# One residue of an output-projection weight block: VectorE subtraction in place of a scaled copy and an adding DMA

## The chip, the cores and the metric

The kernel runs on one core of one Trainium2 chip. The metric is device time in microseconds (us); lower is better. The core has five engines that follow their own instruction streams and meet through semaphores: TensorE (PE in the profile, with its weight loads under PEld), VectorE (DVE), ScalarE (ACT), GpSimd (POOL) and SyncE (SP, which only issues DMAs here). DMAs that SP issues are on the hardware queue q1 in the profile, those that GpSimd issues on the software queue q0.

## What is computed

One layer of a streaming-encoder block on 512 frames of width 1024, all in float32:

```
h = h + 0.5 * swiglu_1(rmsnorm(h))
z = rmsnorm(h) @ w_in          -> conv value, conv gate, q, k, v, r, forget gate
y_conv = silu(layernorm(causal depthwise conv, 31 taps, of value * sigmoid(gate)))
y_gla  = chunked gated linear attention (chunks of 64), normed, gated by silu(r)
h = h + concat([y_conv, y_gla]) @ w_out        # w_out is 1024 x 1024
h = h + 0.5 * swiglu_2(rmsnorm(h))
h = h + sigmoid(rmsnorm(h) @ w_g) * (p @ w_p)
out = rmsnorm(h)
```

The change lies in the preparation of `w_out` for the line in the middle.

## The kernel before, in words

**Three products for one.** To come near float32 accuracy with the faster matmul format `fp32r`, each operand is split in a high part (the value rounded to `fp32r`) and a low part (the value minus the high part, rounded again). A product is then three matmuls: high by high, high by low, low by high (`mm3`, lines 216-219). Each of these takes a 128 x 128 stationary block and a 128 x 512 moving block.

**How a weight becomes two parts.** `load` (171) brings up to 1 MB of weights into one of two buffers named `raw` (shown as `wr`). `high` (178) lets ScalarE cast a 128 x 1024 block of it to the high part, `wh`. The low part, `wl`, is then made in one of two ways:

- `low` (188): VectorE subtracts, `wl = wr - wh`, one instruction.
- `added` (193): ScalarE writes the negated weight to `wl`, and a DMA issued by GpSimd adds `wr` to it in place:

```
act.mul(l3, r3, -1.0)
pool.dma_start(out=l3.bitcast(F32), in_=r3, accum_op=ALU.add)
```

Here `l3` is an `fp32r` tile, so the scaled copy rounds the weight just as the cast for the high part does, and what the DMA adds to it is the unrounded weight. A `raw` buffer is free for its next load when all its readers are done: the casts, the subtractions and the adding DMAs.

**The output projection.** `w_out` is taken in eight column blocks of 128 (n = 0 to 7), loaded two at a time by `oload` (866) in the order 0/1, 4/5, 2/3, 6/7, through the two `raw` buffers in turn. For each block a PSUM bank collects eight products over the rows of `w_out`: rows 4 to 7 meet the attention half `y_gla` (tiles `ygH`, `ygL`), rows 0 to 3 the conv half `y_conv` (tiles `ycH`, `ycL`). `first_part` (882) does the twelve matmuls of rows 4 to 7, for which the conv half isn't needed. Blocks 0, 1, 4 and 5 get their low parts by `added` earlier, blocks 6 and 7 by `low`.

**The order of the work around the change.** From line 520 to line 1007 `in_order(True)` holds PE, DVE and ACT to the order in which the program writes their instructions; POOL and SP take theirs in program order as well. The order is:

1. Lines 925-935: TensorE turns the attention output over into four banks; ScalarE and VectorE split it (`ygH`, `ygL`).
2. Lines 936-937: blocks 2 and 3 of `w_out` are cast and their low parts made, both by `added`. Line 938 loads blocks 6/7, lines 943-944 load `p`.
3. Lines 945-946: `first_part` of blocks 0 and 1.
4. Lines 947-950: VectorE does what is left of the conv taps (shown as `cv<-glu,cw,cv`).
5. Lines 951-955: `first_part` of blocks 4, 5 and 2, with the last two of the matmuls that average the conv output over its channels (`ax<-cv,mean`) put in between.
6. Lines 957-966: VectorE takes the mean off (`cv<-cv,ax`), ScalarE squares (`lnsq`) and casts blocks 6 and 7, VectorE adds up the squares (`lnsq<-lnsq,lnsq`).
7. Line 986: `first_part(3)`, and ahead of its last three matmuls `ln_sums` (968): `colsum` (TensorE, `ax<-ones,lnsq`), then `rsqrt_mean` (251): a scaling on VectorE (`ms`), a power on GpSimd (`rs<-ms,negh`, line 256), and four small VectorE operations (`rs`). While GpSimd is at the power, VectorE is given `low(wo[6])`.
8. Line 987: `first_part(6)`, and ahead of its last three matmuls `ln_out` (971): `spread` (TensorE, `ax<-ident,rs`), then for each of four channel groups a VectorE multiplication (`yc`), the ScalarE activation and cast (`ycH`) and the low part.
9. Lines 999-1011: the rows 0 to 3 of the blocks, which need `ycH`, beginning with blocks 0, 1 and 2.
10. Line 1024: the second feed-forward part, whose first 1 MB weight load goes to the `raw` buffer that held blocks 2/3.

Of the kernel before, what the change touches and what calls it, by code (L numbers as in the profile page):

```python
# [62 lines left out]
def block_kernel(ctx: ExitStack, tc: tile.TileContext, a: dict, out: bass.AP):  # L63
# [33 lines left out]
    def bank():  # L97
        return pp.tile([P, SEQ], F32, tag="mm", bufs=7, name=nm("ps"))
# [36 lines left out]
    def vec(name, c):  # L135
        return vcols[name, c]
# [26 lines left out]
    def gsplit(src, g, s):  # L163
        hi = bt(F32R, s + "H")
        act.activation(hi, src, AF.Copy, scale=g)
        lo = bt(F32R, s + "L")
        dve.scalar_tensor_tensor(out=lo, in0=src, scalar=g, in1=hi.bitcast(F32),
                                 op0=ALU.mult, op1=ALU.subtract)
        return hi, lo
# [18 lines left out]
    def low(w):  # L188
        h3, l3, r3 = w
        dve.tensor_tensor(out=l3, in0=r3, in1=h3.bitcast(F32), op=ALU.subtract)  # L190
        return h3, l3

    def added(w):

        h3, l3, r3 = w
        act.mul(l3, r3, -1.0)
        pool.dma_start(out=l3.bitcast(F32), in_=r3, accum_op=ALU.add)
        return w
# [667 lines left out]
    def oload(n):  # L866
        raw_o[n] = load(a["w_out"][0], 0, DC, n * P, 2 * P)

    def ohigh(n):
        return (high4 if n in (4, 5) else high)(raw_o[n - n % 2][:, :, (n % 2) * P:(n % 2 + 1) * P])  # L870
# [5 lines left out]
    def part(ps, w, ks, first, last, mid={}):  # L876
        for k in ks:
            if k in mid:
                mid[k]()
            mm3(ps, *rows_of(w, k), *mix[k], first and k == ks[0], last and k == ks[-1])  # L880

    def first_part(n, w, mid={}):
        ps = bank()
        part(ps, w, range(4, 8), True, False, mid)
        half[n] = (w, ps)

    oload(0)
    wo, rt = {n: added(ohigh(n)) for n in (0, 1)}, []
# [44 lines left out]
    taps(2)  # L933
    for h in range(4):
        mix[4 + h] = gsplit(yps[h], vec("gla_norm", h), "yg")
    for n in (2, 3):
        wo[n] = added(ohigh(n))
    oload(6)


# [6 lines left out]
    for steps in list(conv):  # L947
        for _ in steps:
            pass
    conv.clear()  # L950
    first_part(4, wo[4])
    pe.matmul(mub, mean, acc[2], start=False, stop=False)
    first_part(5, wo[5])
# [167 lines left out]
```

## Time and profile before

| what | before |
|---|---|
| median of 3 runs | 994.52 us (993.06 to 994.82) |
| the profiled execution, its own time | 994.39 us |
| its span in the trace | 992.7 us |
| mean granted TensorE clock | 0.994 |
| TensorE busy | 974.0 us, 98% |
| VectorE busy | 532.7 us, 54% |
| ScalarE busy | 354.8 us, 36% |
| GpSimd busy | 33.7 us, 3% |

Times in the views are counted from the start of the span; 1.7 us of the execution's time lie outside it. A row of the timeline reads: start, duration, engine, line, operation, output <- inputs, shape, count, and in square brackets the idle time of the engine before it and what ended it. Nearly all engine instructions carry line 46, since a wrapper issues them, so they are known by their tiles.

### The profile page before, as it was taken

What the parts mean: (1) busy time and instruction counts of PE and PEld (TensorE: products, weight loads), DVE (VectorE), ACT (ScalarE), POOL (GpSimd) and SP (SyncE); (2) the same over time, 40 slices, a digit from 0 to 9 for tenths busy, and PEclk for the clock granted to TensorE, in tenths of its full rate; (3) what the DMA queues carried; (4) which work ended last, traced back from release to release, by engine and by line L of the source; (5) the groups of instructions that cost most, each with busy time, mean ns of one, the idle gap of its engine ahead of it and who ended that gap; (6) DMA issues with size and microseconds to landing.
All of it is one profiled execution on the core that took longest, in us unless ns stands there. A gap on an engine that the chain in (4) does not pass through costs nothing.

```text
span 992.7 us, 11176 instructions
## 1 busy us (share of the span) xinstructions
PE 974.0 (98%) x4570; PEld 802.3 (81%) x4570; DVE 532.7 (54%) x755; ACT 354.8 (36%) x539; POOL 33.7 (3%) x44
## 2 busy tenths in 40 slices
PE   7999999999999999999998999999999999999996
PEld 5888888888888888788876888888888888888885
DVE  4655334444434566999985944544333454345454
ACT  5633122332323343454553632322222232233442
POOL 1000000000000000001230000000000000000000
PEclk9999999999999999999998999999999999999999
DMA  6633223322522431125673333232233222133212
GB/s 171 197 122 111 85 85 110 102 85 92 162 86 75 127 96 43 43 86 128 128 112 82 125 114 99 85 99 70 96 117 128 85 85 88 61 101 112 85 44 85
DMA packets 97544, 99.48 MB, mean 100 GB/s; under 512 B 3299, under 2 KB 90933, under 8 KB 97492
## 3 DMA queue, kind: packets, MB, share of 16 engines
q1 hardware_dynamic: 90592, 93.93, 29.5%
q0 software_dynamic: 6720, 4.72, 3.6%
q8 instruction: 36, 0.59, 0.3%
q14 instruction: 16, 0.13, 0.0%
q10 hardware_dynamic: 180, 0.12, 0.0%
HBM read 92.46 MB, written 2.10 MB: 95 GB/s over the span
## 4 chain that ended last, share of the span: by engine, by line
PE 96%; DMA 2%; ACT 1%; DVE 0%; SPq 0%; issue 0%; POOLq 0%; DVEq 0%; ACTq 0%
PE ps L46 95%; DMA wl<-wr 1%; PE ax L46 1%; DMA wr<-in_ffn_w_in 0%; ACT ygH L46 0%; ACT wl L46 0%; ACT wh L46 0%; SPq L150 0%; ACT yc L46 0%; DVE yc L46 0%; ACT hgH L46 0%; POOLq L1117 0%; ACT ycH L46 0%; ACT wa L46 0%; DVE m L46 0%
## 5 line engine op out<-in xcount | busy, mean ns | idle before, releaser
L46 ACT CAST wh<-wr 128x1024 fp32r<-128x1024 f32 (+2 forms) x174 | 172.4, 994 | 442.9 <-PE ps L46 419.3
L46 PE MATMUL ps<-hgH,wh 128*128 128x512 f32 x752 | 293.1, 390 | 0.0
L46 PE MATMUL ps<-hgL,wh 128*128 128x512 f32 x752 | 292.7, 389 | 0.0
L46 PE MATMUL ps<-hgH,wl 128*128 128x512 f32 x752 | 292.6, 389 | 0.0
L46 DVE TENSOR_TENSOR wl<-wr,wh 128x1024 fp32r<-128x1024 f32 (+2 forms) x168 | 192.3, 1147 | 61.6 <-ACT wh L46 61.5
L46 PEld LDWEIGHTS ps<-hgH,wh 128*128 128x128 f32 x752 | 141.1, 188 | 30.1 <-issue 0.8
L46 PEld LDWEIGHTS ps<-hgH,wl 128*128 128x128 f32 x752 | 141.1, 188 | 29.4
L46 PEld LDWEIGHTS ps<-hgL,wh 128*128 128x128 f32 x752 | 141.2, 188 | 29.3 <-DVE hgL L46 0.3
L46 PE MATMUL ps<-actL,wh 128*128 128x512 f32 x352 | 137.0, 389 | 0.0
L46 PE MATMUL ps<-actH,wl 128*128 128x512 f32 x352 | 136.9, 389 | 0.0
L46 PE MATMUL ps<-actH,wh 128*128 128x512 f32 x352 | 136.8, 389 | 0.0
L46 DVE TENSOR_TENSOR u<-ps,bc 128x512 f32<-128x512 f32 x48 | 33.2, 691 | 131.8 <-PE ps L46 131.8
L46 DVE SCALAR_TENSOR_TENSOR cv<-glu,cw,cv 128x504 f32<-128x504 f32 (+25 forms) x120 | 81.3, 733 | 0.6
L46 DVE TENSOR_TENSOR g<-ps,bc 128x512 f32<-128x512 f32 x48 | 33.1, 691 | 86.0 <-PE ps L46 83.1
L46 PEld LDWEIGHTS ps<-actL,wh 128*128 128x128 f32 x352 | 66.1, 188 | 13.9 <-DVE actL L46 0.3
L46 PEld LDWEIGHTS ps<-actH,wh 128*128 128x128 f32 x352 | 66.1, 188 | 13.8
L46 PEld LDWEIGHTS ps<-actH,wl 128*128 128x128 f32 x352 | 66.1, 188 | 13.7
L46 DVE SCALAR_TENSOR_TENSOR h<-ps,h 128x512 f32<-128x512 f32 x40 | 27.7, 692 | 88.9 <-PE ps L46 88.9
L46 PE MATMUL ps<-wh,hgH 128*128 128x512 f32 (+1 forms) x136 | 52.3, 385 | 0.0
L46 PE MATMUL ps<-wl,hgH 128*128 128x512 f32 (+1 forms) x136 | 51.7, 380 | 0.0
L46 PE MATMUL ps<-wh,hgL 128*128 128x512 f32 (+1 forms) x136 | 51.2, 377 | 0.0
L46 ACT ACTIVATE s<-g 128x512 f32<-128x512 f32 x48 | 30.4, 634 | 39.5 <-DVE g L46 35.0
(190 smaller groups left out, 775.1 us busy)
## 6 DMA issues: line engine op xcount, KB each, us to landing
wr<-in_ffn_w_in SPq DMA_DIRECT2D x42, 1024.0 KB, 5.1
wr<-in_w_in SPq DMA_DIRECT2D x10, 1024.0 KB, 5.0
wr<-in_ffn_w_out SPq DMA_DIRECT2D x12, 768.0 KB, 4.5
wr<-in_ffn_w_out SPq DMA_DIRECT2D x8, 1024.0 KB, 5.1
wr<-in_ffn_w_out SPq DMA_DIRECT2D x8, 640.0 KB, 4.1
wr<-in_w_out SPq DMA_DIRECT2D x4, 1024.0 KB
wr<-in_ple_w_gate SPq DMA_DIRECT2D x8, 512.0 KB, 3.4
wl<-wr POOLq DMA_DIRECT2D x6, 512.0 KB, 8.9
```

The lines of the kernel that those rows point to most:

```text
L46: inst = call(*args, **kwargs)
```

## The change

Blocks 2 and 3 were both treated by `added`. Block 2 still is. Block 3 is cast at the same place, and its low part is made by `low`, on VectorE, after the last of the conv taps and ahead of the subtraction of the mean:

```diff
     for h in range(4):
         mix[4 + h] = gsplit(yps[h], vec("gla_norm", h), "yg")
-    for n in (2, 3):
-        wo[n] = added(ohigh(n))
+    wo[2] = added(ohigh(2))
+    wo[3] = ohigh(3)
     oload(6)
...
             pass
     conv.clear()
+    low(wo[3])
     first_part(4, wo[4])
```

Block 3's ScalarE scaling (128 x 1024), its 512 KB adding DMA and the GpSimd issue of it go; one 128 x 1024 VectorE subtraction comes. No other instruction changes its place in any engine's order. `wo[3]` is the same three tiles as before.

## The prediction

> **What bounds the kernel now.** I read the page first: the busy shares and the chain that ended last.
>
> ```profile
> span 992.7 us, 11176 instructions
> PE 974.0 (98%) x4570; PEld 802.3 (81%) x4570; DVE 532.7 (54%) x755; ACT 354.8 (36%) x539; POOL 33.7 (3%) x44
> PE 96%; DMA 2%; ACT 1%; DVE 0%; SPq 0%; issue 0%; POOLq 0%; DVEq 0%; ACTq 0%
> ```
>
> TensorE sets the end. An edit off its path is worth nothing; one that takes a wait of TensorE away is worth the wait. So next the list of what TensorE waited for (total, times, longest), the part of it that lies behind the start-up:
>
> ```profile
> PE ps L46 <- DMA wl<-wr: 2.5, 1, 2.5
> ...
> PE ps L46 <- ACT ycH L46: 1.6, 1, 1.6
> ```
>
> The first is the longest wait of the whole run, and it is for an adding DMA. Then the chain in order of time shows where it is and what stands behind it:
>
> ```profile
> 513.14 13.40 DMA wl<-wr
> ...
> 526.59 2.59 PE ps L46 x7
> ...
> 536.23 0.70 DVE yc L46
> ...
> 538.47 19.35 PE ps L46 x84
> ```
>
> The DMA issued at 513.14 landed 13.4 us later and let TensorE go. Behind it the chain runs through the LayerNorm of the conv half: column sums on TensorE, the reciprocal root, `spread`, the multiplication at 536.23, the activation and cast, and TensorE's restart at 538.47. Which block is it? TensorE's timeline answers:
>
> ```profile
> 521.19 0.39 PE L46 MATMUL ps<-ygH,wl 128*128 128x512 f32 x1
> ...
> 523.47 0.39 PE L46 MATMUL ps<-ygH,wh 128*128 128x512 f32 x1
> 523.69 0.39 PE L46 MATMUL ps<-ygL,wh 128*128 128x512 f32 x1
> 526.59 0.50 PE L46 MATMUL ps<-ygH,wl 128*128 128x512 f32 x1 [2.51 <-DMA wl<-wr]
> ```
>
> Block 2's twelve matmuls begin after the last averaging matmul and end with the one ahead of 523.47; the third matmul of block 3, the first to read its low part, waits. It is the tile that the change makes in another way. From 521.19, the third matmul of block 2, to 523.69 lie 11 starts, so one matmul every 0.2275 us at full clock.
>
> The stall costs more than its 2.51 us. Busy time by stretch (the column behind the engines is the granted clock):
>
> ```profile
> 526.50:527.50 1.00, 0.91 (x4) 0.78 (x5) 0.00 (x0) 0.00 (x0) 0.00 (x0) 1.00 0.00 0
> 527.50:529.00 1.50, 1.50 (x6) 1.11 (x5) 0.00 (x0) 0.00 (x0) 0.00 (x0) 0.51 0.61 180
> ...
> 533.00:534.40 1.40, 1.40 (x5) 1.11 (x4) 0.60 (x4) 0.00 (x0) 0.00 (x0) 0.52 0.00 0
> 534.40:536.00 1.60, 1.60 (x13) 1.44 (x12) 0.00 (x0) 0.00 (x0) 0.00 (x0) 1.00 0.00 0
> ```
>
> And the page's row of the clock, in 40 slices of 24.8 us:
>
> ```profile
> PEclk9999999999999999999998999999999999999999
> ```
>
> About 0.9 us after the restart the clock was halved, and stayed so for 6.9 us (527.5 to 534.4): 3.4 us of lost work, if TensorE alone counted. The one slice below nine tenths (521.2 to 546.0) is the one with the stall.
>
> **The change part by part.** *Removed:* a ScalarE scaling, a GpSimd issue and a 512 KB DMA. The first two save nothing, as both engines wait long behind them (8.81 and 16.27 us):
>
> ```profile
> 511.77 1.08 ACT L46 ACTIVATE wl<-wr 128x1024 fp32r<-128x1024 f32 x1
> 521.65 2.43 ACT L46 ACTIVATE lnsq<-cv 128x512 f32<-128x512 f32 x4 [8.81 <-DVE cv L46]
> 530.96 1.95 POOL L256 TENSOR_TENSOR rs<-ms,negh 128x4 f32<-128x4 f32 x1 [16.27 <-DVE ms L46]
> ```
>
> *Added:* one VectorE subtraction between the last tap and the subtraction of the mean.
>
> ```profile
> 510.00 9.22 DVE L46 SCALAR_TENSOR_TENSOR cv<-glu,cw,cv 128x510 f32<-128x510 f32 x12
> 520.93 2.48 DVE L46 TENSOR_TENSOR cv<-cv,ax 128x512 f32<-128x512 f32 x4 [1.72 <-PE ax L46]
> 523.33 2.28 DVE L46 TENSOR_TENSOR lnsq<-lnsq,lnsq 128x512 f32<-128x512 f32 x3
> 530.71 0.16 DVE L46 TENSOR_SCALAR ms<-ax 128x4 f32<-128x4 f32 x1 [5.10 <-PE ax L46]
> 530.79 1.23 DVE L46 TENSOR_TENSOR wl<-wr,wh 128x1024 fp32r<-128x1024 f32 x1
> 533.54 0.16 DVE L46 TENSOR_TENSOR rs<-rs,rs 128x4 f32<-128x4 f32 x1
> ```
>
> The taps end at 519.22 and VectorE then stands 1.72 us until the average is there. The same operation on the same shape took 1.23 us, so the new one runs from about 519.2 to 520.45 and costs nothing; 0.5 us of the gap stay. Its inputs are there, the cast having ended ahead of 511.77. Queued behind it on VectorE are the mean subtractions and the whole LayerNorm chain; if the gap were gone, that chain would be 1.23 us later. The low part is ready 3.4 us before its matmul, now due at 523.92.
>
> *What is late next.* I follow the path with block 3 unstalled.
>
> - The ninth matmul of block 3 starts at 523.47 + 8 x 0.2275 = 525.29, so the column sums could start at 525.5. They need the squares, added up at 523.33 + 2.28 = 525.61. Start 525.66, 0.15 us of wait.
> - At full clock the sums take less. The same operation earlier in the run:
>
> ```profile
> 378.58 0.95 PE L46 MATMUL ax<-ones,sqacc 128*128 128x1 f32 x8
> 379.39 0.48 PE L46 MATMUL ps<-hgH,wa 128*128 128x512 f32 x1
> 379.56 0.16 DVE L46 TENSOR_SCALAR ms<-ax 128x4 f32<-128x4 f32 x1 [2.02 <-PE ax L46]
> 379.81 1.02 POOL L256 TENSOR_TENSOR rs<-ms,negh 128x4 f32<-128x4 f32 x1 [37.25 <-DVE ms L46]
> ```
>
>   The scaling starts 0.98 us behind the sums: 526.64 in place of 530.71.
> - From the scaling to the end of the last small operation it was 533.70 - 530.71 = 2.99 us. Nothing of that changes (the power on GpSimd and block 6's low part beside it are the same): ready at 529.63, and `spread` can start at 529.7.
> - TensorE meanwhile goes on at 526.47 with three matmuls of block 3 and nine of block 6. The sixth of these twelve reads block 6's low part, which VectorE makes right behind the scaling, 526.72 to 527.95; it would be due at about 527.7 and starts at 528.0. Six more behind it, and TensorE is at `spread` at 529.6. Both arms meet; I take 529.7.
> - Before, `spread` began at 535.14:
>
> ```profile
> 535.14 1.05 PE L46 MATMUL ax<-ident,rs 128*128 128x128 f32 x8
> ```
>
>   It comes 5.4 us earlier. From there to the restart at 538.47 (the 1.6 us wait for `ycH` included) nothing changes.
>
> *Moved:* SyncE's next load, the first of the second feed-forward part, waits for the readers of blocks 2 and 3.
>
> ```profile
> 512.62 0.37 SPq L174 DMA_DIRECT2D wr<-in_w_out  x1
> 513.04 5.57 SPq L944 DMA_DIRECT2D ptok<-in_p  x4
> 526.67 51.10 SPq L174 DMA_DIRECT2D wr<-in_ffn_w_in  x6
> 523.99 1.98 ACT L46 CAST wh<-wr 128x1024 fp32r<-128x1024 f32 x2
> ```
>
> It went right after the landing at 526.54; now it goes when block 2's DMA and the new subtraction are done, about 520.5. It is then in flight beside the load of blocks 6 and 7. In favour, 512 KB of other traffic are gone, and those blocks were loaded before their cast at 523.99, which came straight behind ScalarE's previous work; against, a megabyte joins. At worst its whole transfer (5.1 us, the page's median for such a load) goes ahead of the other's rest: cast of block 6 to 530.2, its low part 531.4, `spread` about 532.3, a gain of 2.9 us in place of 5.4. At best it's nothing. I take nothing, since it is issued 8 us behind the other on the same queue. The load's own earlier arrival is worth nothing: TensorE is busy throughout.
>
> **The sum.** 994.39 (profiled execution) - 5.4 = **989.0 us**. The execution stands 0.13 us under the median of 994.52, which I leave out.
>
> [...]
>
> **The rivals.**
>
> *The clock falls at the next wait.* TensorE still waits 1.6 us for `ycH`, now near 531.4. Against: the same wait, 536.9 to 538.5, left the clock at 1.00. [...] Price 3.4 us: 992.4.
>
> *The slow stretch stays where it is.* Against: it starts just after the only long stall, and no other of the 40 slices is below nine tenths. If it stays, from 527.5 on each matmul takes 0.43 us: block 6's last seven before `spread` bring it to 531.0, and the spreading takes about 0.7 us longer; the multiplication starts at 532.7 in place of 536.23. Gain 3.5: 990.9.
>
> *The LayerNorm chain is longer.* The power took 1.02 us in one row and 1.95 in another; the other GpSimd power of the trace, on 16 columns, took 3.34 us.
>
> ```profile
> 490.17 3.34 POOL L256 TENSOR_TENSOR rs<-ms,negh 128x16 f32<-128x16 f32 x1 [9.04 <-DVE ms L46]
> ```
>
> At 3.34 the gain is 4.0: 990.4. At 1.02 TensorE's own arm binds, and it is 5.5: 988.9. The collision of the loads (991.5) belongs here too.
>
> *Block 2's DMA takes the place of block 3's* (slower). Block 2 stays with the adding DMA:
>
> ```profile
> L197 POOL DMA_DIRECT2D wl<-wr x1: 1557/1557/1557, 511.2 to 511.2; - x1
> DMA to landing us min/median/max: 9.1/9.1/9.1
> ```
>
> It landed at 511.25 + 9.1 = 520.35, 0.84 us ahead of its matmul at 521.19. If it took 13.4 us as the other did, TensorE would stand from 521.2 to 524.7, the clock would fall 0.9 us later, and of the 19 matmuls up to the sums 15 would run at 0.43 us: sums at 532.0, scaling 533.2, `spread` 536.3, 1.15 us later than before: 995.5. It decides from a landing of about 12.2 us on, and from about 14.3 us it is slower by over 0.2%. Against: with block 3's DMA gone it has less traffic beside it.
>
> **How the numbers follow.** Forecast 989.0: 0.75. Clock falls later, 992.4: 0.10. Stretch stays, 990.9: 0.04. Longer chain, 990.4 to 991.5: 0.04. Block 2 late, 995.5: 0.07. What a measurement of this kernel can tell from no change is about 0.2%, 2 us. Faster by more: 0.75 + 0.04 + 0.04 and half of the 0.10, since 992.4 is at the bound: 0.88. Same: the other 0.05 and 0.04 of the last: 0.09. Slower: 0.03. Range: below, 989.0 less 1.4 us, as far as the fastest run (993.06) lies under the median: 987.6; above, 992.4, which takes in the bounds of the load's collision and the power.
>
> **What would show it.** In the changed kernel TensorE has no wait for `wl`; the clock is 1.00 through the output projection; the new subtraction lies between the taps and `cv<-cv,ax` and the latter still waits for TensorE; VectorE's wait ahead of the scaling shrinks from 5.1 to about 1 us; from the restart after `ycH` on, every row is 5.4 us earlier. Wrong would be: a wait of block 2's matmul on its DMA, a clock of 0.5 anywhere behind 521, or a cast of block 6 that waits for its load.

## The result and the profile after

| what | before | after |
|---|---|---|
| median | 994.06 us (991.96 to 994.82, 5 runs) | 989.14 us (988.86 to 989.85, 5 runs) |
| ratio | | 0.9955, 95% interval 0.994 to 0.997 |
| profiled execution, its span | 994.39 us, 992.7 us | 989.85 us, 988.1 us |
| mean granted clock of the profiled execution | 0.994 | 0.998 |

By the ratio the kernel became 0.45% faster; between the medians it is 4.9 us (the ratios in this document are not the quotients of the two medians). 5.4 us, to 989.0, had been forecast. The page of the changed kernel, first its busy shares, then the row of the clock and the shares of the chain that ended last:

```profile
span 988.1 us, 11174 instructions
...
PE 972.3 (98%) x4570; PEld 800.6 (81%) x4570; DVE 533.7 (54%) x756; ACT 353.2 (36%) x538; POOL 32.2 (3%) x43
...
PEclk9999999999999999999999999999999999999999
...
PE 98%; ACT 0%; DVE 0%; DMA 0%; SPq 0%; issue 0%; POOLq 0%; DVEq 0%; ACTq 0%
```

The 2% of the chain that a DMA held are gone, and no slice of the clock is below nine tenths; in every stretch between 517 and 545 us, through the output projection, the granted clock is 1.00. VectorE has one instruction more, ScalarE and GpSimd one less each. From the list of TensorE's waits in the changed kernel (it begins with waits for the first inputs, up to 2.3 us, and the 0.9 us for `wa` ends at 8.07 us; these belong to the start-up):

```profile
PE ps L46 <- ACT ycH L46: 1.6, 1, 1.6
PE ps L46 <- ACT wa L46: 0.9, 1, 0.9
```

The wait for `wl` is no longer in the list; the 1.6 us for `ycH` have stayed. TensorE's timeline of the changed kernel at the places that the forecast named:

```profile
520.58 1.02 PE L46 MATMUL ax<-cv,mean 128*128 128x512 f32 x2
...
521.90 0.39 PE L46 MATMUL ps<-ygH,wl 128*128 128x512 f32 x1
...
524.62 0.39 PE L46 MATMUL ps<-ygH,wl 128*128 128x512 f32 x1
...
526.37 1.05 PE L46 MATMUL ax<-ones,lnsq 128*128 128x1 f32 x8
...
530.60 1.13 PE L46 MATMUL ax<-ident,rs 128*128 128x128 f32 x8
...
534.01 0.50 PE L46 MATMUL ps<-ycH,wh 128*128 128x512 f32 x1 [1.58 <-ACT ycH L46]
```

The second `ygH,wl` here is block 3's first low part, now without a wait. The two spans cannot be laid over each other as they are: the changed kernel reached the last averaging matmul (`ax<-cv,mean`) at 520.58, the one before at

```profile
519.87 1.02 PE L46 MATMUL ax<-cv,mean 128*128 128x512 f32 x2
```

so this execution came 0.71 us later out of the stages ahead, which the change doesn't touch. The difference was there by 16 us: the first `fp32r` matmuls went at the pace of the slow stretch, 0.43 us from start to start, and this lasted until about 13.9 us in the changed kernel and about 12.1 us in the one before (the granted clock in the views shows 1.00 there all the same). So I count from the last averaging matmul to TensorE's restart behind `ycH`. That **stage** took 538.47 - 519.87 = 18.60 us before and 534.01 - 520.58 = 13.43 us after: 5.17 us less. From the restart to the end of the span it is 454.23 us before and 454.09 after: what was gained there was kept.

VectorE's timeline of the changed kernel shows where the new instruction went:

```profile
510.71 9.23 DVE L46 SCALAR_TENSOR_TENSOR cv<-glu,cw,cv 128x510 f32<-128x510 f32 x12
519.85 1.22 DVE L46 TENSOR_TENSOR wl<-wr,wh 128x1024 fp32r<-128x1024 f32 x1
521.64 2.48 DVE L46 TENSOR_TENSOR cv<-cv,ax 128x512 f32<-128x512 f32 x4 [0.57 <-PE ax L46]
524.04 2.28 DVE L46 TENSOR_TENSOR lnsq<-lnsq,lnsq 128x512 f32<-128x512 f32 x3
527.46 0.16 DVE L46 TENSOR_SCALAR ms<-ax 128x4 f32<-128x4 f32 x1 [1.15 <-PE ax L46]
```

It lies in the gap ahead of the mean subtraction, which still waits 0.57 us for TensorE; the scaling `ms` waits 1.15 us for the sums in place of 5.10.

### The profile page after: what moved, and what is told of

It reads as the page before. It is cut to its first block, busy times and chain, and to the rows that moved or that the text cites. A ratio compares the mean times of both kernels' runs of the same rounds, so it can differ in the third digit from the quotient of the medians.

```text
span 988.1 us, 11174 instructions
## 1 busy us (share of the span) xinstructions
PE 972.3 (98%) x4570; PEld 800.6 (81%) x4570; DVE 533.7 (54%) x756; ACT 353.2 (36%) x538; POOL 32.2 (3%) x43
## 4 chain that ended last, share of the span: by engine, by line
PE 98%; ACT 0%; DVE 0%; DMA 0%; SPq 0%; issue 0%; POOLq 0%; DVEq 0%; ACTq 0%
PE ps L46 97%; PE ax L46 1%; DMA wr<-in_ffn_w_in 0%; SPq L150 0%; DVE wl L46 0%; ACT yc L46 0%; DVE ygL L46 0%; DVE yc L46 0%; ACT ygH L46 0%; ACT hgH L46 0%; POOLq L1118 0%; ACT ycH L46 0%; ACT wa L46 0%; DVE m L46 0%; ACT h L46 0%
## 5 line engine op out<-in xcount | busy, mean ns | idle before, releaser
L46 PEld LDWEIGHTS ps<-actH,wl 128*128 128x128 f32 x352 | 66.1, 188 | 13.8
```

The costliest lines, as they stand in the source:

```text
L46: inst = call(*args, **kwargs)
```

## The experiments

Theory: TensorE's wait for block 3's low part cost its own length and, through the idle time, a stretch of half clock; the subtraction is free because of the place it was given. Rivals: the gain comes from the DMA's traffic, or the slow stretch has another cause, or any adding DMA at that place is late. Times are medians; the column before the last is the stage of the profiled execution, counted as above.

| kernel | median (lowest to highest, runs) | ratio to before, 95% interval | stage | clock of its runs |
|---|---|---|---|---|
| late_low | 994.24 (992.74 to 995.26, 12) | 1.0003, 0.9994 to 1.0012 | 18.82 | 0.994 to 0.998 |
| fill | 991.65 (991.00 to 992.70, 12) | 0.9977, 0.9968 to 0.9986 | 16.07 | 0.997 to 0.999 |
| traffic | 989.28 (988.15 to 989.86, 6) | 0.9953, 0.9940 to 0.9967 | 13.43 | 0.997 to 0.998 |
| swap | 988.93 (988.67 to 990.03, 6) | 0.9952, 0.9939 to 0.9965 | 13.43 | 0.997 to 0.998 |
| both_low | 989.23 (989.07 to 989.92, 6) | 0.9958, 0.9944 to 0.9972 | 13.91 | 0.997 to 0.999 |
| early_low | 991.63 (991.22 to 993.84, 12) | 0.9985, 0.9976 to 0.9993 | 16.04 | 0.996 to 0.998 |
| chain | 988.24 (987.58 to 989.09, 6) | 0.9948, 0.9935 to 0.9961 | 12.51 | 0.997 to 0.998 |

The kernel before was run again beside them: 23 runs next to the first four kernels (median 993.61) and 17 next to the last three (993.86).

### late_low: the same stall without a DMA

```diff
     conv.clear()
-    low(wo[3])
     first_part(4, wo[4])
...
         dve.tensor_tensor(out=sqs[0], in0=sqs[0], in1=sqs[c], op=ALU.add)
+    low(wo[3])
```

> The changed kernel with the new subtraction moved behind the adding up of the squares, so that TensorE waits about 2.9 us for block 3's low part with no DMA in it (VectorE 526.2 to 527.5, the matmul due at 524.6 in the changed kernel's trace). Theory (any stall of this length here halves the clock for about 7 us, and the LayerNorm chain takes that over): about 994.5 us, the time of before, with a granted clock of 0.5 for some 7 us behind the restart. Rival (the half clock belongs to the adding DMA or to that place of the program, not to the idle time): the stall alone, delaying the column sums by 2.8 us, about 992.0, clock 1.00.

TensorE's timeline of this kernel, then its stretches:

```profile
519.61 1.02 PE L46 MATMUL ax<-cv,mean 128*128 128x512 f32 x2
...
526.53 0.50 PE L46 MATMUL ps<-ygH,wl 128*128 128x512 f32 x1 [2.72 <-DVE wl L46]
...
538.43 0.51 PE L46 MATMUL ps<-ycH,wh 128*128 128x512 f32 x1 [1.58 <-ACT ycH L46]
```

```profile
525.00:527.00 2.00, 0.47 (x2) 0.43 (x3) 1.48 (x2) 0.69 (x1) 0.00 (x0) 1.00 0.00 0
527.00:528.00 1.00, 1.00 (x6) 0.76 (x5) 0.00 (x0) 0.00 (x0) 0.00 (x0) 0.85 0.23 50
528.00:528.50 0.50, 0.50 (x3) 0.40 (x2) 0.00 (x0) 0.00 (x0) 0.00 (x0) 0.50 0.82 211
...
533.00:534.00 1.00, 1.00 (x4) 0.81 (x3) 0.39 (x3) 0.00 (x0) 0.00 (x0) 0.50 0.00 0
534.00:535.00 1.00, 1.00 (x5) 0.82 (x4) 0.00 (x0) 0.00 (x0) 0.00 (x0) 0.73 0.00 0
```

The wait is now for VectorE, 2.72 us, and the clock is halved from about 527.7 to 534.5, again some 6.8 us. The whole gain is gone (ratio 1.0003) though block 3's adding DMA is gone too. So the half clock does not belong to the DMA, and a VectorE subtraction as such buys nothing. The wait lies at the same matmul as before, so this run alone doesn't tell the idle time from that place of the program; the next one does.

### fill: the wait covered with matmuls

```diff
+    def fill():
+        ps = aux()
+        wh, _ = rows_of(wo[0], 4)
+        for i in range(FILL):
+            pe.matmul(ps, wh, mix[4][0], start=(i == 0), stop=(i == FILL - 1))
+
+    FILL = 12
-    first_part(3, wo[3], {7: ln_sums})
+    first_part(3, wo[3], {4: fill, 7: ln_sums})
```

It starts from the kernel of before.

> The kernel of before, with 12 more matmuls (2.7 us at full clock, result not used) ahead of block 3's first, so that TensorE is busy while it would wait for the adding DMA. Theory (stall and half clock are two costs, the second caused by the idle time): the low part still comes at about 526.5, the clock stays at 1.00, spread is reached about 2.8 us earlier than in before: about 991.2 us. Rival (the slow stretch has another cause and stays): about 994, no change. Rival (the stall's 2.5 us are all there is): about 994, no change in time although the clock stays at 1.00.

TensorE's timeline of this kernel:

```profile
520.12 1.02 PE L46 MATMUL ax<-cv,mean 128*128 128x512 f32 x2
...
523.71 3.01 PE L46 MATMUL ax<-ygH,wh 128*128 128x512 f32 x12
526.56 0.39 PE L46 MATMUL ps<-ygH,wh 128*128 128x512 f32 x1
...
527.02 0.40 PE L46 MATMUL ps<-ygH,wl 128*128 128x512 f32 x1
...
532.79 1.13 PE L46 MATMUL ax<-ident,rs 128*128 128x128 f32 x8
...
536.19 0.50 PE L46 MATMUL ps<-ycH,wh 128*128 128x512 f32 x1 [1.58 <-ACT ycH L46]
```

Block 3's low part is used no earlier (527.02), and yet the kernel with twelve useless matmuls is 2.0 us faster between the medians, its clock 0.997 or more in all 12 runs. With TensorE kept busy at the same place, the half clock doesn't come: it follows the idle time. The stage (536.19 - 520.12 = 16.07 us) tells the two costs apart: 18.60 - 16.07 = 2.5 us for the half clock, 16.07 - 13.43 = 2.6 us for the wait itself, or here for the twelve matmuls in its place. Both rivals that foresaw no change fall.

### traffic: the removed work put back, unread

```diff
     wo[3] = ohigh(3)
+    idle = [bt(F32R, "idle").rearrange("p (k c) -> p k c", k=4) for _ in range(2)]
+    for i in range(2):
+        act.mul(idle[i], wo[3][2][:, 4 * i:4 * i + 4], -1.0)
+        pool.dma_start(out=idle[i].bitcast(F32), in_=wo[3][2][:, 4 * i:4 * i + 4], accum_op=ALU.add)
```

> The changed kernel, and beside it the removed work again: block 3 is scaled on ScalarE and added by DMA (two of 256 KB) into tiles that nobody reads. Theory (only TensorE's wait cost time; the traffic, ScalarE's 1.1 us and GpSimd's issue are free): about 989.1 us, within 0.1% of the changed kernel, and the first load of the second feed-forward part goes out about 5 us later than in the changed kernel at no cost. Rival (the freed DMA time, ScalarE time or the earlier load carries part of the gain): 991 to 994.

Measured 989.28 us, and the stage is the changed kernel's to the hundredth (13.43). SyncE's timeline of traffic, then that of the changed kernel:

```profile
527.26 12.32 SPq L174 DMA_DIRECT2D wr<-in_ffn_w_in  x2
```

```profile
521.10 19.36 SPq L174 DMA_DIRECT2D wr<-in_ffn_w_in  x2
```

The two added DMAs took 10.9 and 13.8 us, the longer one about as long as block 3's before. The first load of the second feed-forward part went out 6.2 us later by the spans' clocks, 7.0 us counted from the last averaging matmul (519.69 us in traffic), at no cost. The traffic, ScalarE's and GpSimd's share and the earlier load carry nothing of the gain.

### swap: block 3 keeps the DMA, alone

```diff
-    wo[2] = added(ohigh(2))
-    wo[3] = ohigh(3)
+    wo[2] = ohigh(2)
+    wo[3] = added(ohigh(3))
...
-    low(wo[3])
+    low(wo[2])
```

> Block 2 by the VectorE subtraction and block 3 by the adding DMA: one adding DMA in place of two, and the block that waited keeps it. Theory (block 3's DMA took 13.4 us because it stood behind block 2's; alone it takes about 9): issued near 512.9, landed near 522, ahead of its matmul at 524.6; no wait, about 989.1 us. Rival (13.4 us come from the loads of w_out and p beside it): landed near 526.3, a wait of about 1.7 us and perhaps a half clock, 991 to 994.

The view of the tile `wl` around the issue, in this kernel:

```profile
L197 POOL DMA_DIRECT2D wl<-wr x1: 1557/1557/1557, 512.1 to 512.1; - x1
...
DMA to landing us min/median/max: 10.9/10.9/10.9
```

TensorE's timeline, block 3's first matmul that reads the low part:

```profile
523.80 0.39 PE L46 MATMUL ps<-ygH,wl 128*128 128x512 f32 x1
```

Alone it took 10.9 us, between the 9.1 of block 2's and the 13.4 of block 3's in the kernel before, and landed at about 523.0, ahead of its matmul. So 2.5 us of the 13.4 go when the other adding DMA goes, and 1.8 us more than block 2's stay. That fits a part for both theories but doesn't show it: the DMA also went out earlier here, 0.4 us ahead of the load of `w_out` (512.50) where it had been 0.5 us behind it (512.62), and the two weren't tried apart. The time is that of the changed kernel (988.93 against 989.14). It is enough that one of the two adding DMAs goes; that it was block 3's isn't needed.

### both_low: the second subtraction doesn't fit

```diff
-    wo[2] = added(ohigh(2))
+    wo[2] = ohigh(2)
     wo[3] = ohigh(3)
...
+    low(wo[2])
     low(wo[3])
```

> The changed kernel with block 2 made by VectorE too, so two subtractions between the taps and the mean subtraction and no adding DMA here. Theory (the gap on VectorE holds one subtraction and not two; what goes over it stands on the path): in the changed kernel 0.57 us of the gap were left, the second takes 1.13 to 1.22, so the LayerNorm chain comes 0.6 us later: about 989.7 us, no clock below 1.00, and block 2's matmuls don't wait. Rival (block 2's DMA still costs something that the trace doesn't show): below 989.0.

VectorE's timeline of this kernel, and TensorE's:

```profile
519.45 2.35 DVE L46 TENSOR_TENSOR wl<-wr,wh 128x1024 fp32r<-128x1024 f32 x2
521.73 2.47 DVE L46 TENSOR_TENSOR cv<-cv,ax 128x512 f32<-128x512 f32 x4
```

```profile
526.45 1.05 PE L46 MATMUL ax<-ones,lnsq 128*128 128x1 f32 x8 [0.48 <-DVE lnsq L46]
```

The gap ahead of the mean subtraction is used up, and the column sums wait 0.48 us for VectorE; the stage is 0.48 us longer than the changed kernel's, where 0.6 had been expected. The medians differ by 0.09 us and don't resolve that; the trace does.

### early_low: the same subtraction, ahead of the taps

```diff
     oload(6)
+    low(wo[3])
...
     conv.clear()
-    low(wo[3])
     first_part(4, wo[4])
```

> The changed kernel with the subtraction ahead of the last twelve taps in place of behind them. Theory (the place is what makes it free): VectorE, held to its order, waits for ScalarE's cast of block 3 (to 512.6 in the changed kernel's trace, VectorE being free at 510.7) and then subtracts, so the taps come 3.0 us later, TensorE waits for them at the two averaging matmuls (about 0.7 and 1.7 us) and the LayerNorm chain is 2.4 us later: about 991.5 us; should the clock fall to a half on these two waits, up to 994.5. Rival (any place ahead of block 3's matmul does): 989.1.

VectorE's timeline of this kernel, and TensorE's:

```profile
511.88 1.23 DVE L46 TENSOR_TENSOR wl<-wr,wh 128x1024 fp32r<-128x1024 f32 x1 [1.84 <-ACT wh L46]
```

```profile
519.57 0.39 PE L46 MATMUL ps<-ygH,wa 128*128 128x512 f32 x1
522.31 1.12 PE L46 MATMUL ax<-cv,mean 128*128 128x512 f32 x2 [2.35 <-DVE cv L46]
```

Held to its order, VectorE waits 1.84 us for ScalarE's cast, and the taps come 3.1 us later, counted from the first of the two averaging matmuls (516.21 us here, 516.98 in the changed kernel). That one didn't have to wait; TensorE waited only at the second, 2.35 us. Its due time was 519.57 + 0.23 = 519.80, and the stage from there to the restart at 535.84 is 16.04 us, 2.6 more than the changed kernel's. The time (991.63) was forecast; the two waits were one. The clock stayed up in 11 of 12 runs; the one at 993.84 us had 0.996.

### chain: what binds next

```diff
-        lln.append(rsqrt_mean(colsum([sqs[0]]), D_CONV, TB, between=lambda: low(wo[6])))
+        sums = colsum([sqs[0]])
+        low(wo[6])
+        lln.append(rsqrt_mean(sums, D_CONV, TB))
...
-    first_part(6, wo[6], {7: ln_out})
+    first_part(6, wo[6], {6: ln_out})
```

> The changed kernel with block 6's subtraction ahead of the scaling in place of beside GpSimd's power, and the spreading three matmuls earlier in block 6. Theory (after the change the path is bound by the LayerNorm chain: the power is longer beside a VectorE subtraction, 1.96 against 1.02 us elsewhere, and TensorE loses 0.3 us at block 6's low part): the power near 1.0, no wait for that low part, spread about 0.8 us earlier, TensorE's wait for the cast shorter but still there: about 988.3 us, faster than the changed kernel. Rival (TensorE's own work sets it and the chain has slack): 989.1 or somewhat above.

GpSimd's and TensorE's timelines of this kernel:

```profile
526.42 1.03 POOL L256 TENSOR_TENSOR rs<-ms,negh 128x4 f32<-128x4 f32 x1 [14.18 <-DVE ms L46]
```

```profile
531.81 0.50 PE L46 MATMUL ps<-ycH,wh 128*128 128x512 f32 x1 [0.90 <-ACT ycH L46]
```

The power took 1.03 us in place of 1.96, and the wait for `ycH` is 0.90 us in place of 1.58. The stage is 12.51 us, 0.92 shorter than the changed kernel's; the median, 988.24 us, is 0.9 below it. The intervals of the two ratios overlap, so the times alone don't separate them; the stage agrees with the medians in size. The edit does two things, the power without a subtraction beside it and the earlier spreading; what each is worth wasn't tried. Its median is the lowest of the table.

## Why the prediction was right, and how far

- **The stall and its tile**: as forecast; removed by the change, reproduced by late_low without the DMA.
- **The subtraction costs nothing**: a gap of 0.5 us was to stay, 0.57 stayed. both_low and early_low show what it costs without that cover, 0.48 and 2.6 us of stage.
- **What is late next**, counted from the last averaging matmul: column sums forecast at 5.79 us (525.66 - 519.87), measured 5.79; scaling 6.77, measured 6.88; `spread` 9.83, measured 10.02; restart 13.16 (18.60 less the 5.44 us by which `spread` was to come earlier), measured 13.43. The differences add up to 0.27 us: the sums took 1.05 us in place of 0.95, `spread` started 0.15 us behind its input (530.45) in place of 0.07 (in chain, where TensorE stood ready for it, it was 0.14) and took 1.13 us in place of 1.05.
- **The earlier load**: taken at nothing, and traffic shows that it is nothing; block 6's cast came straight behind ScalarE's previous work again (524.69). The forecast's worst case, `spread` at 532.3, was too mild by its own count: it followed VectorE and left out TensorE's seven matmuls behind the low part at 531.4, which end at about 533.0, a gain of 2.1 us and not 2.9. That case didn't come up.
- **Block 2's DMA**: the rival needed over 12.2 us; it landed after 8.9.
- **The clock at the `ycH` wait**: the rival had 0.10. In the changed kernel, traffic, swap, both_low and chain together, 29 runs, no clock was below 0.997. That wait was 0.90 us in chain and 1.6 us in the others.
- **The size**: the term mis-sized is the slow stretch. The forecast took it as belonging to every execution of the kernel before, as the one trace showed. It doesn't. Of the 40 runs of before beside the experiments, 9 had a mean clock of 0.998, and these took 991.46 to 992.25 us (median 992.0); the other 31 had 0.994 to 0.996 and took 992.72 to 996.01 (median 994.2); the four at 0.996, 992.72 to 993.55 us, lie nearest to the first group, and no trace shows such a run. A stretch of 6.9 us at half clock lowers the mean over 990 us by 0.0035, about the difference between the two groups. So the kernel before ran in two ways, one with the wait alone, about 2.9 us over the changed kernel's 989.14, and one with the half clock as well, 2.2 us more. The trace shows the second; for the first it is worked out from clocks and times, and from fill. fill, which removes only the half clock, has nearly the first group's time (991.65 against 992.0). The forecast was made against an execution of the second group, so it held for that one (5.17 us of stage against 5.4); over all runs the gain is smaller by the share of the first. That the median of the changed kernel then lay within 0.2 us of 989.0 is partly luck: its own runs spread over 1.0 us.

The sentence in the forecast that every row behind the restart would be 5.4 us earlier failed in its wording: they are 4.46 us earlier by the span's clock, since the changed kernel's execution was 0.71 us behind before the stage began. Differences of a stage have to be taken from a common event.

## What to carry to other kernels

Look for the longest wait of the engine that sets the end, then ask two things of a cure: where the new work stands on its engine (the same 1.2 us subtraction was worth 5, 2 or 0 us by its place), and what else the wait costs besides its length, here a half-speed stretch about as dear as the wait (2.5 and 2.6 us of stage, by fill). A profile is one draw: when the granted clock of the runs falls in two groups (here 0.998 in 9 runs of 40 and 0.994 to 0.996 in 31), the profiled execution belongs to one of them, and the gain over the median is a mixture.

## What the runs showed of the hardware

Whether the clock fell at a wait of TensorE varied from run to run, and in these runs it fell more often the longer the wait was; a mean clock below 0.997 is taken as the sign. At the 1.58 us wait for `ycH` it never fell in the 23 runs of the changed kernel, traffic, swap and both_low. With a wait of 2.35 us (early_low) 1 run of 12 was below 0.997, with 2.51 us (before) 31 of 40, with 2.72 us (late_low) 11 of 12; the waits are those of the profiled executions. The two longest lie at the same matmul, the others at other places, so length and place aren't wholly told apart. In the two traces that show it (before and late_low) the half clock came 0.9 and 1.2 us after the restart and lasted 6.9 and 6.8 us, while TensorE was busy.

The power on GpSimd in the LayerNorm chain took 1.95 to 1.96 us in every trace in which block 6's VectorE subtraction ran beside it, and 1.03 us in chain, on the same data, where it didn't.
